# Order of narrow products, a later value product, and two reordered loads in a two-layer encoder

## The chip, the cores and the metric

The kernel runs on one core of a Trainium2 chip. The metric is the device time of one execution in microseconds (us); lower is better. The time before is 1998.18 us, the median of three runs.

## The reference, cut to what matters

256 tokens of width 2048 pass through two layers. Each layer has a token mixer, four cross-attention heads into 256 memory tokens, an output projection and a squared-ReLU MLP of width 8192. All data is float32.

```
m = rms_norm(mem, mem_norm); h = x
for i in range(2):
    n = rms_norm(h, attn_norm[i])
    if i == 0:   q, k, v, qm = split(n @ a_w_in)   # 12 heads, neighbourhood attention + bias
    else:        q, k, v, qm = split(n @ b_w_in)   # 12 query heads on 4 key/value heads,
                                                   # q, k RMS-normed per head, then rotary
    km, vm = split(m @ w_mem_kv[i])                # 4 cross-attention heads
    h = h + concat(mix, cross) @ w_o[i]
    n = rms_norm(h, mlp_norm[i])
    h = h + square(relu(n @ w_up[i])) @ w_down[i]
return rms_norm(h, final_norm)
```

In the first layer each query sees all 4 grid rows and 16 of the 64 columns. The kernel reorders the tokens column by column, so that the 128 queries of a row tile need only 160 neighbouring keys. These are the narrow heads.

## The kernel before, in words

**Numbers.** Every float32 operand is split in two: `hi` is the value rounded by ScalarE to the matrix engine's format (fp32r), `lo` is the rest, computed by VectorE (`split`, lines 484 to 487). A product of two operands is three matmuls: hi x hi, hi x lo, lo x hi.

**Work and its units.** Weights come in chunks of 1 MB, and each chunk is worked off in two half chunks (`halves_of`). There are two kinds. In an S chunk the weights are the stationary operand and a product streams 256 columns (`products`, line 391, 24 products a half chunk, sums `ps_s`, or `ps_u` in the MLP). In an M chunk the activations are stationary and a product streams 512 columns (`m_products`, lines 368, 371, 372, 12 products a half chunk, sums `ps_m`). For each half chunk ScalarE and VectorE make `hi` and `lo` from `raw`, the loaded weights.

**Order.** `run_all` goes through the half chunks one by one. A counter, `tick`, advances after each, and `later(n, f)` runs `f` that many half chunks on; so the attention steps are put in between the projection products. Loads and splits are issued some half chunks ahead. The order in which the functions issue their instructions is then rearranged for each engine by the framework's own scheduler, which works with simulated times and data dependences. `pin` keeps a DMA or instruction in program order; `issue_after(x)` holds what is issued inside it behind instruction `x`. Each engine executes its own queue in order.

**First layer.** The stage begins with the memory's keys and values of both layers. Meanwhile `x_load` (line 826) loads x into `h` and x transposed into two `xT` tiles, four transfers on SyncE's queue. `x_norm` converts xT into `nT` (ScalarE line 516, VectorE line 517, 16 each), and `x_stats` (line 835) squares x on ScalarE and sends the inverse norms around by DMA as `x_row`. Then come the four cross-attention query heads, and three groups of four narrow heads. A group is one value block (4 M chunks) and then a query chunk and a key chunk (S) for each head. When the key chunk of a head is done, `a_k_done` plans the head's steps: scores (`attend_near`), turning the probabilities (`turned_near`), splitting them (`halved`), and the value product (`attend3_near`) 1, 2, 4 and 6 half chunks later. Scores and value product are two pairs of matmuls each: one with 320 columns (both halves of the moving operand, hi as weights) and one with 160 (hi moving, lo as weights), that add up in the same sum. The last head's value product has three 160-column matmuls instead of a pair.

**Second layer.** Queries come in three blocks of four heads (`b_q_done`). `normed_heads` norms them and applies the rotary positions, for the two row tiles i = 0, 1 of 128 tokens: ScalarE scales (lines 1482, 1488), VectorE does six operations (lines 1490, 1496, 1498). TensorE then transposes the result (`heads_T`, line 1453), and scores, softmax (`attend`, with the reciprocal in line 553) and value products of the heads follow, in between products of the output projection.

Of the kernel before, what the change touches and what calls it, by code (L numbers as in the profile page):

```python
# [14 lines left out]
ALU = mybir.AluOpType  # L15
# [143 lines left out]
def encoder_kernel(ctx: ExitStack, tc: tile.TileContext, t: dict, out: bass.AP):  # L159
# [374 lines left out]
    def attend(qT, kT):  # L534
        kT = kT if isinstance(kT, Far) else Near(kT)
        sc_ps = at.att.tile([P, NT, SEQ], F32, tag="att", name="sc_ps")
        for s in range(NT):
            i = NT - 1 - s
            qh, ql = qT[:, i * P : (i + 1) * P], qT[:, SEQ + i * P : SEQ + (i + 1) * P]
            kh, kl = kT.part(0), kT.part(1)  # L540
            ps = kT.out(sc_ps[:, s, :])
            nc.tensor.matmul(ps, qh, kh, start=True, stop=False)  # L542
            nc.tensor.matmul(ps, qh, kl, start=False, stop=False)  # L543
            nc.tensor.matmul(ps, ql, kh, start=False, stop=True)  # L544
        sc = at.work.tile([P, NT, SEQ], F32, tag="sc", bufs=3 + box["layer"], name="sc")
        nm = small.tile([P, NT], F32, tag="nm", name="nm")
        sm = small.tile([P, NT], F32, tag="sm", name="sm")
        nc.vector.tensor_reduce(nm, sc_ps, axis=AX.X, op=ALU.max, negate=True)
        for s in range(NT):
            nc.scalar.activation(sc[:, s, :], sc_ps[:, s, :], AF.Exp, bias=nm[:, s : s + 1],  # L550
                                 accum_out=sm[:, s : s + 1])
        rs = small.tile([P, NT], F32, tag="rs", name="rs")
        nc.vector.reciprocal(rs, sm)
        for s in range(NT):
            nc.vector.tensor_scalar(sc[:, s, :], sc[:, s, :], rs[:, s : s + 1], None, op0=ALU.mult)
        return sc
# [44 lines left out]
    def attend_near(q, k, bias):  # L601

        kk = k.rearrange("p (b t) -> p b t", b=2)
        sc = at.work.tile([P, NT, NEAR], F32, tag="sc", bufs=3, name="sc")
        nm = small.tile([P, NT], F32, tag="nm", name="nm")
        sm = small.tile([P, NT], F32, tag="sm", name="sm")
        for i in range(NT):
            ps = at.att.tile([P, 2, SEQ], F32, tag="att", name="sc_ps")
            s = slice(i * STEP, i * STEP + NEAR)
            nc.tensor.matmul(ps[:, :, :NEAR], q[:, i * P : (i + 1) * P], kk[:, :, s], start=True, stop=False)  # L610
            nc.tensor.matmul(ps[:, 0, :NEAR], q[:, SEQ + i * P : SEQ + (i + 1) * P], kk[:, 0, s], start=False, stop=True)
            nc.vector.tensor_tensor(sc[:, i, :], ps[:, 0, :NEAR], bias[:, i * NEAR : (i + 1) * NEAR], op=ALU.add)
            nc.vector.tensor_tensor(sc[:, i, :], ps[:, 1, :NEAR], sc[:, i, :], op=ALU.add)
        nc.vector.tensor_reduce(nm, sc, axis=AX.X, op=ALU.max, negate=True)
        for i in range(NT):
            nc.scalar.activation(sc[:, i, :], sc[:, i, :], AF.Exp, bias=nm[:, i : i + 1], accum_out=sm[:, i : i + 1])
        rs = small.tile([P, NT], F32, tag="rs", name="rs")
        nc.vector.reciprocal(rs, sm)
        for i in range(NT):
            nc.vector.tensor_scalar(sc[:, i, :], sc[:, i, :], rs[:, i : i + 1], None, op0=ALU.mult)  # L620
        return sc
# [26 lines left out]
    def attend3_near(pT, v, head, cat):  # L648
        av = at.att.tile([P, 2, SEQ], F32, tag="att", name="av")
        for k in range(NT):  # L650
            q, s = slice(k * STEP, k * STEP + NEAR), slice(k * NEAR, (k + 1) * NEAR)
            if head < NH - 1:
                nc.tensor.matmul(av[:, :, q], v(0, k), pT[:, :, s], start=k == 0, stop=False, skip_group_check=True)
            else:
                for n in range(2):
                    nc.tensor.matmul(av[:, 0, q], v(0, k), pT[:, n, s], start=k == n == 0, stop=False,
                                     skip_group_check=True)
            box["av"] = nc.tensor.matmul(av[:, 0, q], v(1, k), pT[:, 0, s], start=False, stop=k == NT - 1,
                                         skip_group_check=True)
        if head == NH - 1:  # L660
            box["cat", head] = split(cat[:, head, :SEQ], cat[:, head, SEQ:], av[:, 0, :])
            return
        y = at.work.tile([P, SEQ], F32, tag="av_s", name="av_s")
        nc.scalar.activation(y, av[:, 1, :], AF.Copy)
        nc.vector.tensor_tensor(y, av[:, 0, :], y, op=ALU.add)
        box["cat", head] = split(cat[:, head, :SEQ], cat[:, head, SEQ:], y)
# [157 lines left out]
        along_free(box["mem_col"], box["mem_row"])  # L824

    def x_load():
        for i in range(NT):
            pin(nc.sync.dma_start(h[:, i, :], t["x"][i * P : (i + 1) * P, :]))
        box["xT"] = []
        for a in range(2):  # L830
            y = at.work.tile([P, 8, SEQ], F32, tag="l4", name="xT")
            pin(nc.sync.dma_start(y.rearrange("p a b -> p (a b)"), t["xT"][:, a * XW // 2 : (a + 1) * XW // 2]))
            box["xT"].append(y)

    def x_stats():
        ss = small.tile([P, NT], F32, tag="ss0", name="x_ss")
# [36 lines left out]
    def a_k_done(hd):  # L873
        def f(w):
            k = at.work.tile([P, 512], F32R, tag="b_y2", name="kT")
            s = summed(w.ps, "k", box["x_row"])
            split(k[:, :SEQ], k[:, SEQ:], s)
            b = at.work.tile([P, NT * NEAR], F32, tag="b_o", bufs=3, name="bias")
            nc.sync.dma_start(b, t["bias"][hd])
            attention([(box.pop(("q", hd)), k, b, head_of(box["v", hd // GH], hd % GH), hd, box["cat"])], 1,  # L880
                      steps=(0, 1, 3, 5 if hd < NH - 1 else 4))
        return f

    def a_qm_done(hd):
# [587 lines left out]
        hi, lo = (dst[:, :, n * SEQ : (n + 1) * SEQ].rearrange("p k (c j) -> p k c j", j=32) for n in range(2))  # L1472
        split(hi, lo, box["q_raw"].rearrange("p t a k j -> p k (t a) j"))

    def normed_heads(w):
        cg, sg = box["rope"]
        outs = []
        for i in range(NT):
            y2 = at.work.tile([P, 4, HD], F32, tag="b_y2", name="b_y2")
            ss = small.tile([P, 4], F32, tag="b_ss", name="b_ss")  # L1480
            for j in range(4):
                nc.scalar.activation(y2[:, j, :], w.ps[i][:, j * HD : (j + 1) * HD], AF.Square,
                                     scale=box["rstd"][:, i : i + 1], accum_out=ss[:, j : j + 1])
            r = rstd_of(ss, HD, "b_r")
            nc.gpsimd.tensor_scalar(r, r, box["rstd"][:, i : i + 1], None, op0=ALU.mult)
            y = at.work.tile([P, 4, HD], F32, tag="b_y", name="b_y")
            for j in range(4):
                nc.scalar.activation(y[:, j, :], w.ps[i][:, j * HD : (j + 1) * HD], AF.Copy, scale=r[:, j : j + 1])
            o = at.work.tile([P, 4, HD], F32, tag="b_o", bufs=2, name="b_o")
            nc.vector.tensor_tensor(o, y, cg[:, i, None, :].to_broadcast([P, 4, HD]), op=ALU.mult)  # L1490
            yv = y.rearrange("p h (a b c) -> p h a b c", a=2, b=2)
            y2v = y2.rearrange("p h (a b c) -> p h a b c", a=2, b=2)
            sv = sg[:, i, :].rearrange("p (a b c) -> p a b c", a=2, b=2)
            for a in range(2):
                for b in range(2):
                    nc.vector.tensor_tensor(y2v[:, :, a, b, :], yv[:, :, a, 1 - b, :],
                                            sv[:, None, a, b, :].to_broadcast([P, 4, 32]), op=ALU.mult)
            nc.vector.tensor_tensor(o, o, y2, op=ALU.add)
            outs.append(o.rearrange("p a b -> p (a b)"))
        return outs  # L1500

# [11 lines left out]

    def b_q_done(blk):
        def f(w):
            outs = normed_heads(w)
            qT = at.work.tile([P, 4, 512], F32R, tag="l4", name="qT1")
            if blk == 0:
                later(1, queries_far, outs)
                later(3, queries_split, qT)  # L1520
            else:
                later(1, heads_T, outs, 4, qT)
            kvs = [(blk * 4 + j) // (NH // NKV) for j in range(4)]
            attention([(qT[:, j, :], Far(box["kT"], kv), None, head_of(box["vb"], kv), blk * 4 + j, box["cat"])
                       for j, kv in enumerate(kvs)], 1 if blk else 3, 2, (0, 3, 6) if blk else (0, 2, 5, 6),
                      2 if blk == 2 else 0)
# [44 lines left out]
    later(21, x_load)  # L1571
    for j in range(8):
        later(24 + j, x_norm, j)
    later(25, x_stats)
    run_all()
    assert not pending, pending
    closed(*reversed(list(pools)))
# [148 lines left out]
```

## Time and profile before

| | |
|---|---|
| median of 3 runs | 1998.18 us (1997.32 to 1998.4) |
| profiled execution, whole | 1997.71 us |
| profiled execution, span from first to last instruction | 1995.6 us |
| TensorE products | busy 1987.0 us, 12870 products |
| TensorE weight loads | busy 1805.0 us |
| VectorE | busy 1717.4 us |
| ScalarE | busy 1327.9 us |
| mean granted TensorE clock | 0.999 |

Engines in the profile are PE (TensorE products), PEld (its weight loads, one for each product, that run beside the products), DVE (VectorE), ACT (ScalarE), POOL (GpSimd) and SP (SyncE, which only issues DMAs). L391 is line 391 of the kernel. A row of the timeline has the start, the time, engine, line, operation, output and inputs, shapes and a count; matmuls are pipelined, so the time from one start to the next says what a product costs, and its own duration is longer than that. The shapes of a product end in its moving columns (128x320).

### The profile page before, as it was taken

Reading aid. Unit: us, or ns where it says so; the run is one execution under the profiler, and the core shown is the slowest. Engines: PE = TensorE matmul, PEld = TensorE weight load, DVE = VectorE, ACT = ScalarE, POOL = GpSimd, SP = SyncE. Lnnn points to the kernel's source line nnn. Section 1 sums busy time; section 2 is a strip of 40 time slices with the busy share of each in tenths; the row PEclk is TensorE's granted clock in tenths of the full one; section 3 lists DMA queues with packets and bytes.
Section 4 is the critical chain, followed back from the end, with each engine's and each line's share of the span. In section 5 each row is a group of like instructions: output and inputs, shape, how many; then the busy total and the mean of one; then the engine's idle time right before and its main releaser. Section 6 shows DMA issues by size and latency. Waiting matters only on the chain.

```text
span 1995.6 us, 32767 instructions
## 1 busy us (share of the span) xinstructions
PE 1987.0 (100%) x12870; PEld 1805.0 (90%) x12870; DVE 1717.4 (86%) x2147; ACT 1327.9 (67%) x1860; POOL 138.2 (7%) x179
## 2 busy tenths in 40 slices
PE   9999999999999999999999999999999999999998
PEld 8999999899999999999998888889999999999997
DVE  7777767589898999999999779778998999999997
ACT  6655555477777777677676656667776777777674
POOL 0000000000000000000000001000000000000000
PEclk9999999999999999999999999999999999999999
DMA  7856555767777777777766764567777777777772
GB/s 294 317 195 201 198 192 184 265 200 233 239 232 226 232 232 237 237 227 231 213 227 209 261 223 150 197 192 259 228 223 240 224 229 236 235 236 227 226 234 107
DMA packets 112731, 446.42 MB, mean 224 GB/s; under 512 B 24128, under 2 KB 45376, under 8 KB 65216
## 3 DMA queue, kind: packets, MB, share of 16 engines
q1 hardware_dynamic: 94560, 413.02, 59.0%
q0 software_dynamic: 17728, 30.78, 9.6%
q8 instruction: 101, 1.65, 0.3%
q10 hardware_dynamic: 288, 0.52, 0.1%
q14 instruction: 54, 0.44, 0.1%
HBM read 397.78 MB, written 4.19 MB: 201 GB/s over the span
## 4 chain that ended last, share of the span: by engine, by line
PE 98%; ACT 1%; DVE 0%; issue 0%; DMA 0%; SPq 0%; DVEq 0%; POOLq 0%; POOL 0%; ACTq 0%
PE ps_u L391 35%; PE ps_s L391 9%; PE p L1183 9%; PE p L1181 9%; PE p L1184 9%; PE ps_m L371 8%; PE ps_m L372 8%; PE ps_m L368 8%; DVE nT L517 0%; PE sc_ps L544 0%; PE sc_ps L543 0%; PE sc_ps L542 0%; PE av L679 0%; PE av L678 0%; PE av L680 0%
## 5 line engine op out<-in xcount | busy, mean ns | idle before, releaser
L391 PE MATMUL ps_u<-hT,uh 128*128 128x256 f32 x3812 | 663.6, 277 | 0.0
L391 PEld LDWEIGHTS ps_u<-hT,uh 128*128 128x128 f32 x3812 | 579.1, 188 | 5.5
L391 PE MATMUL ps_u<-hT,ul 128*128 128x256 f32 x1960 | 542.2, 277 | 0.0
L486 ACT ACTIVATE uh<-raw_U 128x1024 fp32r<-128x1024 f32 x262 | 276.7, 1058 | 205.5 <-PE ps_u L391 192.6
L391 PEld LDWEIGHTS ps_u<-hT,ul 128*128 128x128 f32 x1960 | 368.2, 188 | 0.0
L487 DVE TENSOR_TENSOR lo<-raw,hi 128x1024 fp32r<-128x1024 f32 (+1 forms) x215 | 254.0, 1188 | 92.1 <-ACT hi L486 91.2
L487 DVE TENSOR_TENSOR ul<-raw_U,uh 128x1024 fp32r<-128x1024 f32 x262 | 318.3, 1219 | 14.9 <-ACT uh L486 14.8
L487 DVE TENSOR_TENSOR tl<-t,th 128x2048 fp32r<-128x2048 f32 x116 | 265.6, 2289 | 71.9 <-ACT th L486 71.5
L486 ACT ACTIVATE hi<-raw 128x1024 fp32r<-128x1024 f32 (+1 forms) x215 | 221.7, 1037 | 157.4 <-PE ps_m L372 87.1
L486 ACT ACTIVATE th<-t 128x2048 fp32r<-128x2048 f32 x116 | 222.7, 1920 | 118.8 <-PE p L1184 115.6
L487 DVE TENSOR_TENSOR bl<-b,bh 128x1536 fp32r<-128x1536 f32 x116 | 203.1, 1751 | 0.0
L1181 PE MATMUL p<-th,a_s 128*128 128x512 f32 x464 | 181.4, 391 | 0.0
L1183 PE MATMUL p<-tl,a_s 128*128 128x512 f32 x464 | 181.1, 390 | 0.0
L1184 PE MATMUL p<-th,a_s 128*128 128x512 f32 x464 | 180.7, 389 | 0.0
L1150 POOL DMA_DIRECT2D t<-b x116 | 100.6, 868 | 1144.3 <-ACT t L1149 1060.9
L486 ACT ACTIVATE bh<-b 128x1536 fp32r<-128x1536 f32 x116 | 172.4, 1486 | 7.8
L391 PE MATMUL ps_s<-nT,hi 128*128 128x256 f32 x896 | 155.9, 279 | 0.0
L1184 PE MATMUL p<-bh,a_s 128*128 128x512 f32 x348 | 136.3, 392 | 0.0
L391 PEld LDWEIGHTS ps_s<-nT,hi 128*128 128x128 f32 x896 | 135.8, 188 | 0.2
L1183 PE MATMUL p<-bl,a_s 128*128 128x512 f32 x348 | 135.8, 390 | 0.0
L1181 PE MATMUL p<-bh,a_s 128*128 128x512 f32 x348 | 135.6, 390 | 0.0
L391 PE MATMUL ps_s<-nT,lo 128*128 128x256 f32 x448 | 125.3, 280 | 0.0
(312 smaller groups left out, 3585.6 us busy)
## 6 DMA issues: line engine op xcount, KB each, us to landing
raw_U<-in_w_up SPq DMA_DIRECT2D x128, 1024.0 KB, 5.9
b<-in_w_pair SPq DMA_DIRECT2D x116, 1024.0 KB, 5.8
raw<-in_w_o SPq DMA_DIRECT2D x32, 1024.0 KB, 5.0
t<-b POOLq DMA_DIRECT2D x116, 256.0 KB, 5.2
raw<-in_w_b SPq DMA_DIRECT2D x21, 1024.0 KB, 5.2
raw<-in_w_av SPq DMA_DIRECT2D x12, 1024.0 KB, 5.0
raw<-in_w_aq SPq DMA_DIRECT2D x12, 1024.0 KB, 5.0
raw<-in_w_ak SPq DMA_DIRECT2D x12, 1024.0 KB, 4.9
```

Source lines behind the costliest of these rows:

```text
L368: first = nc.tensor.matmul(ps, ah, hi[:, s], start=st, stop=False)
L371: nc.tensor.matmul(ps, ah, lo[:, s], start=False, stop=False)
L372: final = nc.tensor.matmul(ps, al, hi[:, s], start=False, stop=sp)
L391: ins = nc.tensor.matmul(ps, x, acts[:, k, part], start=k == n == 0, stop=k == KT - 1 and n == 2)
L486: first = nc.scalar.activation(dst_hi, src, AF.Copy)
L487: return first, nc.vector.tensor_tensor(dst_lo, src, dst_hi.bitcast(F32), op=ALU.subtract)
L1150: nc.gpsimd.dma_start(s[:, 3, :], b[:, 1, :], accum_op=ALU.add)
L1181: ins = nc.tensor.matmul(ps, a[:, 0, ai, :], hi[:, s], start=begins, stop=False)
L1183: nc.tensor.matmul(ps, a[:, 0, ai, :], lo[:, s], start=False, stop=False)
L1184: nc.tensor.matmul(ps, a[:, 1, ai, :], hi[:, s], start=False, stop=ends)
```

## The change

Four edits:

1. In `attend_near` and `attend3_near` the 160-column product of each pair is issued before the 320-column one, and now begins the sum. (In the last head it goes before the two that replace the 320-column one.)
2. The value product of heads 3 and 7, the last of a group, comes 10 half chunks after the key chunk and not 6. Head 11 keeps its place.
3. `x_load` issues the two transfers of xT before the two of x, and `x_stats` is planned for tick 28, not 25.
4. In the last query block of the second layer the six rotary operations of row tile 1 on VectorE are held behind the reciprocal that was issued last, the one of head 7's softmax.

```diff
 def attend(...)
-        nc.vector.reciprocal(rs, sm)
+        box["divided"] = nc.vector.reciprocal(rs, sm)
 def attend_near(...)
-            nc.tensor.matmul(ps[:, :, :NEAR], q[:, i * P : (i + 1) * P], kk[:, :, s], start=True, stop=False)
-            nc.tensor.matmul(ps[:, 0, :NEAR], q[:, SEQ + i * P : SEQ + (i + 1) * P], kk[:, 0, s], start=False, stop=True)
+            nc.tensor.matmul(ps[:, 0, :NEAR], q[:, SEQ + i * P : SEQ + (i + 1) * P], kk[:, 0, s], start=True, stop=False,
+                             skip_group_check=True)
+            nc.tensor.matmul(ps[:, :, :NEAR], q[:, i * P : (i + 1) * P], kk[:, :, s], start=False, stop=True,
+                             skip_group_check=True)
 def attend3_near(...)
+            nc.tensor.matmul(av[:, 0, q], v(1, k), pT[:, 0, s], start=k == 0, stop=False, skip_group_check=True)
             if head < NH - 1:
-                nc.tensor.matmul(av[:, :, q], v(0, k), pT[:, :, s], start=k == 0, stop=False, skip_group_check=True)
+                box["av"] = nc.tensor.matmul(av[:, :, q], v(0, k), pT[:, :, s], start=False, stop=k == NT - 1,
+                                             skip_group_check=True)
             else:
                 for n in range(2):
-                    nc.tensor.matmul(av[:, 0, q], v(0, k), pT[:, n, s], start=k == n == 0, stop=False,
-                                     skip_group_check=True)
-            box["av"] = nc.tensor.matmul(av[:, 0, q], v(1, k), pT[:, 0, s], start=False, stop=k == NT - 1,
-                                         skip_group_check=True)
+                    box["av"] = nc.tensor.matmul(av[:, 0, q], v(0, k), pT[:, n, s], start=False,
+                                                 stop=k == NT - 1 and n == 1, skip_group_check=True)
 def x_load()
-        for i in range(NT):
-            pin(nc.sync.dma_start(h[:, i, :], t["x"][i * P : (i + 1) * P, :]))
         box["xT"] = []
         ...
+        for i in range(NT):
+            pin(nc.sync.dma_start(h[:, i, :], t["x"][i * P : (i + 1) * P, :]))
 def a_k_done(hd)
-                      steps=(0, 1, 3, 5 if hd < NH - 1 else 4))
+                      steps=(0, 1, 3, 4 if hd == NH - 1 else 9 if hd % GH == GH - 1 else 5))
-    def normed_heads(w):
+    def normed_heads(w, behind=None):
         ...
+            with tc.issue_after(behind.ins) if behind and i else nullcontext():
+                turned_by_place()        # the six rotary operations, as before
 def b_q_done(blk)
-            outs = normed_heads(w)
+            outs = normed_heads(w, box["divided"] if blk == 2 else None)
 ...
-    later(25, x_stats)
+    later(28, x_stats)
```

More of the change, by code (lines that the diff above doesn't have):

```diff
@@ L1489, in normed_heads, with turned_by_place @@
             o = at.work.tile([P, 4, HD], F32, tag="b_o", bufs=2, name="b_o")
[L1490 to L1498, printed above, removed]
+            def turned_by_place():
+                nc.vector.tensor_tensor(o, y, cg[:, i, None, :].to_broadcast([P, 4, HD]), op=ALU.mult)
+                yv = y.rearrange("p h (a b c) -> p h a b c", a=2, b=2)
+                y2v = y2.rearrange("p h (a b c) -> p h a b c", a=2, b=2)
+                sv = sg[:, i, :].rearrange("p (a b c) -> p a b c", a=2, b=2)
+                for a in range(2):
+                    for b in range(2):
+                        nc.vector.tensor_tensor(y2v[:, :, a, b, :], yv[:, :, a, 1 - b, :],
+                                                sv[:, None, a, b, :].to_broadcast([P, 4, 32]), op=ALU.mult)
+                nc.vector.tensor_tensor(o, o, y2, op=ALU.add)
+            with tc.issue_after(behind.ins) if behind and i else nullcontext():
+                turned_by_place()
             outs.append(o.rearrange("p a b -> p (a b)"))
```

## The prediction

> **What bounds the kernel now.** I read the page first: busy time, then the chain that ended last.
>
> ```profile
> span 1995.6 us, 32767 instructions
> PE 1987.0 (100%) x12870; PEld 1805.0 (90%) x12870; DVE 1717.4 (86%) x2147; ACT 1327.9 (67%) x1860; POOL 138.2 (7%) x179
> PE 98%; ACT 1%; DVE 0%; issue 0%; DMA 0%; SPq 0%; DVEq 0%; POOLq 0%; POOL 0%; ACTq 0%
> ```
>
> TensorE is never out of work for more than a moment: the chain is 98% its own. So an edit counts only where it changes how long a product takes or where a product waits. The change touches the first layer's narrow heads (144 to 355 us), the load of x (54 to 80 us) and the last query block of the second layer (1220 to 1280 us); the two MLPs hold most of the span and stay as they are. What can be won is what the products there lose against their best rhythm.
>
> The second view is the chain in order of time in the narrow heads' stage. Each row is an uninterrupted run of projection products (256 columns): start, time, count.
>
> ```profile
> 94.89 9.07 PE ps_s L391 x80
> 144.34 15.87 PE ps_s L391 x140
> 160.69 10.93 PE ps_s L391 x96
> 172.74 11.22 PE ps_s L391 x95
> 185.32 5.60 PE ps_s L391 x49
> 214.30 16.49 PE ps_s L391 x140
> 243.33 11.22 PE ps_s L391 x95
> 284.89 16.49 PE ps_s L391 x140
> ```
>
> Divide time by count. The same instruction has two rhythms: 113.4 ns (15.87/140), 113.9 and 114.3, against 118.1 (11.22/95) and 117.8 (16.49/140). A run keeps its rhythm to the end. The borders between runs are the narrow heads' products, and there the timeline of the PE shows what changes it:
>
> ```profile
> 171.87 0.24 PE L611 MATMUL sc_ps<-kT,qT 128*128 128x160 f32 x1
> 171.94 0.32 PE L391 MATMUL ps_s<-nT,lo 128*128 128x256 f32 x1
> 172.10 0.31 PE L653 MATMUL av<-pT_n,va 128*128 128x320 f32 x1
> 172.24 0.24 PE L658 MATMUL av<-pT_n,va 128*128 128x160 f32 x1
> 172.32 0.35 PE L653 MATMUL av<-pT_n,va 128*128 128x320 f32 x1
> 172.50 0.24 PE L658 MATMUL av<-pT_n,va 128*128 128x160 f32 x1
> 213.79 0.24 PE L658 MATMUL av<-pT_n,va 128*128 128x160 f32 x1
> 213.87 0.43 PE L372 MATMUL ps_m<-hi,nT 128*128 128x512 f32 x1
> 214.14 0.28 PE L391 MATMUL ps_s<-nT,lo 128*128 128x256 f32 x1
> ```
>
> Read starts, not durations. A 320-column product takes 0.14 (172.10 to 172.24), a 160-column one 0.07 (172.24 to 172.32), but the product behind a 160-column one is about 0.04 late: 320 columns take 0.18 (172.32 to 172.50), 256 columns 0.16 (171.94 to 172.10), 512 columns 0.27 (213.87 to 214.14). The weight loads say why:
>
> ```profile
> 172.25 0.19 PEld L653 LDWEIGHTS av<-pT_n,va 128*128 128x128 f32 x1
> 172.36 0.19 PEld L658 LDWEIGHTS av<-pT_n,va 128*128 128x128 f32 x1
> ```
>
> These two loads enclose the 160-column product of 172.24 and start 0.11 apart: 0.07 of product cannot hide 0.11 of load. What follows the lateness is the slow rhythm: after the block at 172.5 the next 95 products run at 118 ns, and the run of 140 behind the late 512-column product of 213.87 does too, while the run of 140 at 144.34, with no narrow block ahead, runs at 113.4.
>
> **The change part by part**, against the profiled execution's own 1997.71 us (1995.6 of span and 2.1 around it). The median of the runs, 1998.18, is 0.47 above it; I add that at the end. A measurement of this kernel tells about 0.2%, 4.0 us, from no change.
>
> *160-column products first.* No product, load or transfer is added. A block goes from 320, 160, 320, 160 to 160, 320, 160, 320: still two products behind a 160-column one, two times 0.04, so the direct cost is the same. What can change is the rhythm afterwards, because a late 320-column product now stands last, where a late projection product followed. Best case: no run behind a block is slow, and the three runs of 95 (one in each group of four heads) fall from 11.22 to about 10.82 (95 x 113.9 ns): -1.2. Worst: a late wide product hands the slow rhythm on, as the 512-column one at 213.87 did; then the runs of 96 and of 49 become slow too, (96 + 49) x 4.2 ns x 3 = +1.8. The nearest row is 213.87, a wide product as well, which speaks for the loss; but of the three places where projection products directly follow a block (160.5, 172.6, 185.2) only one stayed slow, so the order of the products after it decides as well. I take 0 and keep both ends.
>
> The Trainium skill (TensorE: Matmul & The Clock Gate, section LDWEIGHTS) puts a load at its 128 columns over 1.2 GHz, 107 ns; the 0.11 between the two load rows agrees. By that rule alone a 160-column product uncovers its successor's load wherever it stands, and this edit gives 0.
>
> *A group's last value product four half chunks on.* Heads 3 and 7. Their four products, ScalarE's copy, VectorE's sum and the split into `cat` move; nothing else is queued for them before the output projection, and the value tile they read is asked for again only a group later. The block stands one product ahead of the first projection run (213.4 to 213.9). Four half chunks of 24 products later it falls about 96 products into that run of 140. The first 96 then start behind undisturbed 512-column products, as at 144.34: (16.49 - 15.87)/140 = 4.4 ns each, 0.42 a run, 0.85 for two. If the remaining 44 stay fast as well it is 0.62 a run, 1.24. A gain of nothing, if something other than the block makes those runs slow, is kept as a rival. I take -1.0.
>
> *Transposed input first.* Four 1 MB transfers swap places on SyncE's queue; nothing is added. The stall that this concerns is at 78 us:
>
> ```profile
> L828 SPq DMA_DIRECT2D first<-in_x x2: 477/606/734, 54.4 to 55.2; - x2
> L832 SPq DMA_DIRECT2D xT<-in_xT x2: 473/522/572, 55.7 to 56.3; - x2
> DMA to landing us min/median/max: 10.7/11.6/12.5
> L525 POOL DMA_DIRECT2D x_row<-rows x4: 720/721/743, 72.4 to 74.6; - x4
> L516 ACT ACTIVATE nT<-xT,first 128x256 fp32r<-128x256 f32 x16 | 6.5, 495 | 0.0
> L840 ACT ACTIVATE sq<-first 128x512 f32<-128x512 f32 x8 | 4.9, 618 | 0.0
> 76.22 2.00 ACT L486 ACTIVATE hi<-raw 128x1024 fp32r<-128x1024 f32 x2
> 77.47 2.34 DVE L487 TENSOR_TENSOR lo<-raw,hi 128x1024 fp32r<-128x1024 f32 x2
> 77.94 0.62 PE L368 MATMUL ps_m<-hi,memT 128*128 128x512 f32 x2
> 78.73 0.50 PE L371 MATMUL ps_m<-lo,memT 128*128 128x512 f32 x1 [0.17 <-DVE lo L487]
> ```
>
> Two products start from 77.94 at the usual 0.23, so the next was due at 78.40; it starts at 78.73 and takes 0.50, not 0.39: about 0.45 lost. It waited for `lo`, that for `hi` at 76.22, which stood in ScalarE's queue behind the 16 conversions of xT. xT first lets these begin earlier; the squares of x come after them, with three half chunks more until they are due. Gain between 0.45 (conversions out of the way) and 0 (the eight squares take their place ahead of the same `hi`; VectorE, which has no squares, still finds `lo` sooner). A loss is bounded by the row of inverse norms: its transfers were issued at 72.4 to 74.6, and it is first used behind the projection products that begin at 94.9; three half chunks of 24 products, some 2.7 us each, leave about 10 us. I take -0.3.
>
> *Last rotary products held.* VectorE's rotary work of the last query block's second half (row tile i = 1) must now follow the reciprocal of head 7:
>
> ```profile
> 1231.56 0.68 DVE L1490 TENSOR_TENSOR b_o<-b_y,cos_q 128x512 f32<-128x512 f32 x1
> 1232.16 0.68 DVE L1496 TENSOR_TENSOR b_y<-b_y,sin_q 128x128 f32<-128x128 f32 x3
> 1234.39 1.21 DVE L487 TENSOR_TENSOR lo<-raw,hi 128x1024 fp32r<-128x1024 f32 x1
> 1235.59 0.68 DVE L1498 TENSOR_TENSOR b_o<-b_o,b_y 128x512 f32<-128x512 f32 x1
> 1235.65 0.50 PE L371 MATMUL ps_m<-lo,cat 128*128 128x512 f32 x1
> 1250.26 0.17 DVE L553 RECIPROCAL rs<-sm 128x2 f32<-128x2 f32 x1 [0.22 <-ACT sc L550]
> 1252.10 2.39 DVE L487 TENSOR_TENSOR lo<-raw,hi 128x1024 fp32r<-128x1024 f32 x2 [0.69 <-ACT hi L486]
> 1252.19 0.60 PE L1453 MATMUL pt_h<-ident,b_o 128*128 128x128 f32 x4
> ```
>
> Gain: the `lo` of 1234.39 ends just before TensorE's product of 1235.65, which takes about 0.11 more than 0.39. Without 1.4 us of rotary products ahead of it that wait goes: -0.1, and it is all there is to win. Cost: the six operations (0.68, four within 0.9, 0.68: about 2.2) start after 1250.4 and end near 1252.6 at best; the transposes that read them stand at 1252.19, 0.4 late. At worst they stand behind the two `lo` of 1252.10 and the transposes come at 1256.2, 4.0 late. Queued behind the held work on VectorE are those two `lo`; behind the transposes the scores, softmax and value products of heads 8 to 11. TensorE meanwhile has output-projection products of finished heads, as in this stretch now. I take 0 for the cost, with 4.0 as the other end.
>
> Sum: 0 - 1.0 - 0.3 - 0.1 = -1.4: 1996.3 in a profile, 1996.8 as a median.
>
> **The rivals.**
>
> *The new order clears every run.* For it: the runs that start after blocks recover in two cases of three. Against it: 213.87. -1.2 - 1.24 - 0.45 - 0.1 = -3.0: median 1995.2.
>
> *A late wide product hands the slow rhythm on.* For it: 214.14 behind 213.87. +1.8 - 0.85 - 0.3 - 0.1 = +0.55: median 1998.7.
>
> *The rhythm does not hang on the blocks*, so the two edits on them do nothing: -0.4, median 1997.8. The Trainium skill (SBUF — State Buffer, section Who interferes with whom) gives TensorE two independent read ports and says that it waits on nobody; by that, the two read streams could not disturb each other. The rows of 113.4 and 117.8 ns for one instruction are not explained by it, so it gets little.
>
> *The held rotary work delays the last heads* (slower). Place: transposes at 1252.19. Price: up to 4.0, with the other gains kept 1997.7 - 1.4 + 4.0 = 2000.3, median 2000.8; without them 2002.2. It decides once the delay exceeds the output products that TensorE has ready beside the last heads; up to that point it costs nothing.
>
> **How the numbers follow.** Chances: forecast 0.43, all runs cleared 0.22, rhythm handed on 0.17, no effect 0.08, rotary delay 0.10. The range leaves out half of the rotary case and the far end of the clearing one: 1994.8 to 1999.8. Faster by over 4.0 us needs under 1994.2, 1.0 below the best case: 0.06. Slower by as much needs the full rotary delay and no gain: 0.05. The rest, 0.89, is no difference that can be told.
>
> **What would show it.** The chain's runs from 214 and 285 us should read 96 products at 113.4 ns each, with a narrow block behind them; if they stay at 118, the second edit failed. Runs of 95 at 118 again: order neutral; at 114: the clearing rival; runs of 96 or 49 at 118: the handing-on one. At 78 us no product should start late. TensorE should show no wait on the split of `qT` or on `cat` between 1250 and 1282; a wait there, or a schedule that reorders the products in some other place, makes the forecast wrong.

## The result and the profile after

| | before | after |
|---|---|---|
| median of 22 runs each | 1998.36 us | 1994.92 us |
| lowest to highest | 1997.31 to 1999.45 | 1993.94 to 1996.71 |
| ratio, 95% interval | | 0.9984 (0.9978 to 0.999) |
| profiled execution, whole | 1997.71 us | 1995.76 us |

The kernel is 3.4 us faster (0.17%). That is real, since the interval ends below 1, but it is inside the 4 us that the prediction counted as no change. The forecast of 1996.8 was 1.9 us too high; the range (1994.8 to 1999.8) held by only 0.12 us. Page of after, busy time and chain:

```profile
span 1993.9 us, 32782 instructions
PE 1984.5 (100%) x12870; PEld 1802.1 (90%) x12870; DVE 1715.7 (86%) x2147; ACT 1327.4 (67%) x1860; POOL 137.4 (7%) x179
PE 99%; DMA 0%; issue 0%; ACT 0%; SPq 0%; DVE 0%; DVEq 0%; POOLq 0%; POOL 0%; ACTq 0%
```

The same 12870 products now keep TensorE busy 2.5 us less. So the gain is in how long products take, not in work. To find the place, I cut three executions at the same TensorE products (first product with x, first query product and so on) and took the difference of their starts. The third column is a second profile of the changed kernel, e5 below.

| stage, us | before | after | after, e5 |
|---|---|---|---|
| first product to first M product | 23.16 | 23.50 | 23.05 |
| rest of the memory's keys and values | 66.30 | 65.83 | 65.83 |
| cross-attention queries, first value block | 49.45 | 49.45 | 49.45 |
| narrow heads, later value blocks | 187.75 | 186.39 | 185.65 |
| output projection | 88.87 | 88.89 | 88.89 |
| MLP | 660.32 | 660.30 | 660.10 |
| second layer's mixer and output | 246.62 | 246.49 | 246.49 |
| MLP | 660.38 | 660.39 | 660.38 |
| end | 7.49 | 7.50 | 7.49 |

Three stages moved, and they are those that the edits touch: 0.47, 2.10 (e5) and 0.13. The first MLP is scatter: it takes 660.10 to 660.69 over the fourteen profiles of this study, whatever edits they have. The first line varies without any reason in the code: from 22.87 to 24.09 over the same profiles. The stages must therefore be compared, and not the spans. The narrow heads' stage repeats well: 187.75 in before, e3, e4 and e9, which have the same code there. Line numbers of after are a little higher: the 160-column products are L610 (scores) and L654 (values), the 320-column ones L612 and L656.

The chain of after in order of time, narrow heads, runs of 256-column products (start, time, count):

```profile
144.11 14.51 PE ps_s L391 x128
158.81 1.20 PE ps_s L391 x10
160.29 9.78 PE ps_s L391 x86
172.49 9.53 PE ps_s L391 x84
184.69 5.68 PE ps_s L391 x50
213.27 2.73 PE ps_s L391 x24
216.51 11.80 PE ps_s L391 x104
286.94 11.80 PE ps_s L391 x104
```

Divide again: 113.4, 113.7, 113.5, 113.6, 113.8, 113.5. No long run at 118 ns is left. Two further things are new. Each pair of projection runs has a run of 10 between (120 ns each, with one late product in it), and the value product of the heads 3 and 7 stands 24 products into its run, not 96. The timeline of PE between 169.9 and 172.5 shows what the runs of 10 are:

```profile
169.90 0.35 PE L610 MATMUL sc_ps<-kT,qT 128*128 128x160 f32 x2
170.09 0.32 PE L391 MATMUL ps_s<-nT,lo 128*128 128x256 f32 x1
171.28 0.46 PE L612 MATMUL sc_ps<-kT,qT 128*128 128x320 f32 x2
171.58 0.23 PE L654 MATMUL av<-pT_n,va 128*128 128x160 f32 x1
171.65 0.44 PE L391 MATMUL ps_s<-nT,hi 128*128 128x256 f32 x2
171.93 0.31 PE L656 MATMUL av<-pT_n,va 128*128 128x320 f32 x1
172.07 0.24 PE L654 MATMUL av<-pT_n,va 128*128 128x160 f32 x1
172.15 0.35 PE L656 MATMUL av<-pT_n,va 128*128 128x320 f32 x1
172.33 0.28 PE L391 MATMUL ps_s<-nT,lo 128*128 128x256 f32 x1
172.45 0.39 PE L391 MATMUL ps_s<-nT,hi 128*128 128x256 f32 x2
```

A block is no longer one piece. The 160-column product streams only `hi`, which ScalarE makes first; put first in its pair, it no longer waits for VectorE's `lo`, and the scheduler issues it earlier: two score products ten projection products ahead of the other two, a value product two to four ahead. The last product of the block is the late 320-column one (172.15 to 172.33, 0.18), and the projection products behind it run at 113.5.

The two other places, timelines of after. At 78 us, where `lo` had been waited for, products follow each other at 0.22 to 0.23:

```profile
78.18 0.61 PE L368 MATMUL ps_m<-hi,memT 128*128 128x512 f32 x2
78.63 0.39 PE L371 MATMUL ps_m<-lo,memT 128*128 128x512 f32 x1
78.86 0.39 PE L372 MATMUL ps_m<-hi,memT 128*128 128x512 f32 x1
```

And in the second layer VectorE makes the third `lo` of that stretch without row tile 1's rotary work ahead of it; the held work and the transposes come later:

```profile
1231.59 0.13 DVE L553 RECIPROCAL rs<-sm 128x2 f32<-128x2 f32 x1
1231.63 1.21 DVE L487 TENSOR_TENSOR lo<-raw,hi 128x1024 fp32r<-128x1024 f32 x1
1249.68 0.69 DVE L1502 TENSOR_TENSOR b_o<-b_o,b_y 128x512 f32<-128x512 f32 x1
1252.69 0.82 PE L1455 MATMUL pt_h<-ident,b_o 128*128 128x128 f32 x6
```

The waits of PE have no row between 1248 and 1284 us. One wait is there that before's profile did not have:

```profile
252.94 0.46 PE L612 MATMUL sc_ps<-kT,qT 128*128 128x320 f32 x2
253.33 0.47 ACT L486 ACTIVATE pT_n<-pT_n 128x320 fp32r<-128x320 f32 x1 [3.89 <-DMA pT_n<-sc_t]
253.85 0.34 PE L654 MATMUL av<-pT_n,va 128*128 128x160 f32 x1 [0.46 <-ACT pT_n L486]
```

Head 6's turned probabilities came late by DMA, and TensorE lost 0.73 us here. This is why the narrow heads' stage of after is longer than that of e5, which has no such wait. The first of these transfers took 5.2 us from issue to landing, and 3.1 in e5, which is the same program. Nor is the wait the change's own: e2 and e10 below keep the old order of the blocks and wait here too (1.06 and about 0.5).

### The profile page after: what moved, and what is told of

The parts are those of the page before. It is cut to its first block, busy times and chain, and to the rows that moved or that the text cites. A ratio compares the mean times of both kernels' runs of the same rounds, so it can differ in the third digit from the quotient of the medians.

```text
span 1993.9 us, 32782 instructions
## 1 busy us (share of the span) xinstructions
PE 1984.5 (100%) x12870; PEld 1802.1 (90%) x12870; DVE 1715.7 (86%) x2147; ACT 1327.4 (67%) x1860; POOL 137.4 (7%) x179
## 4 chain that ended last, share of the span: by engine, by line
PE 99%; DMA 0%; issue 0%; ACT 0%; SPq 0%; DVE 0%; DVEq 0%; POOLq 0%; POOL 0%; ACTq 0%
PE ps_u L391 35%; PE ps_s L391 10%; PE p L1185 9%; PE p L1183 9%; PE p L1186 9%; PE ps_m L368 8%; PE ps_m L372 8%; PE ps_m L371 8%; PE sc_ps L544 0%; PE sc_ps L543 0%; PE sc_ps L542 0%; PE av L681 0%; PE av L682 0%; PE av L680 0%; DMA first<-in_mem_rest 0%
```

## Experiments

The stages and runs below come from one profile of each kernel. The times of e1 to e7 are medians of eleven runs, beside the median of before's. e8 to e12 ran once each (1998.45, 1998.27, 1999.05, 1999.80 and 2000.01 us, with 1998.32, 1997.28 for three of them, and 1998.50 for before beside them); these times tell nothing alone, and only the profiles are read.

**e1, edit 1 alone.** Before with the new order in `attend_near` and `attend3_near`, nothing else.

> Edit 1 alone. Theory A (a narrow block that ends in a 160-column product leaves the slow rhythm of 118 ns behind, one that ends in a 320-column product does not, so this edit alone cures the runs of 95 and the runs of 140 behind the value product of heads 3 and 7): all projection runs between 144 and 331 us at 113.4 to 114 ns, 2.4 us less than before in the time. Rival B (each edit has its own share: this one cures only the three runs of 95, the move of the value product cures the two runs of 140): 1.2 us less, and the runs of 140 still at 118 ns.

1996.99 us against 1997.83 (ratio 0.9996, 0.9987 to 1.0005). The intervals of e1 to e4 all include 1, so what each edit is worth is read from its stage. The narrow heads' stage: 186.81, 0.94 less. Its chain:

```profile
143.91 14.51 PE ps_s L391 x128
172.29 9.54 PE ps_s L391 x84
213.60 15.08 PE ps_s L391 x128
283.87 15.08 PE ps_s L391 x128
```

The run that was the one of 95 is fast (113.6). The runs behind the value blocks of heads 3 and 7 stay slow (117.8), new order or not. So edit 1 does nearly half of the stage's gain. Where a projection product directly follows the late 320-column product, nothing is handed on. Ahead of the two runs at 117.8 ns, two 512-column products stand between. Timeline of PE:

```profile
212.79 0.35 PE L656 MATMUL av<-pT_n,va 128*128 128x320 f32 x1
212.98 0.39 PE L371 MATMUL ps_m<-lo,nT 128*128 128x512 f32 x1
213.21 0.39 PE L372 MATMUL ps_m<-hi,nT 128*128 128x512 f32 x1
213.44 0.28 PE L391 MATMUL ps_s<-nT,lo 128*128 128x256 f32 x1
```

The 320-column product takes 0.185 here as well, and the two behind it 231 and 230 ns, by the unrounded starts; the two ahead of the run that starts at 143.75 (113.4 ns) take 227 and 226. So here the block's lateness may have been handed on through them; no run separates that from the mere nearness of the block to the border.

**e2, edit 2 alone.**

```diff
-                      steps=(0, 1, 3, 5 if hd < NH - 1 else 4))
+                      steps=(0, 1, 3, 4 if hd == NH - 1 else 9 if hd % GH == GH - 1 else 5))
```

> Edit 2 alone. In the instruction order the block of heads 3 and 7 now stands behind the first 24 projection products of the run, with the 320-column product still ahead of its 160-column one, and the projection goes on with a product on hi weights, as at 172.5 us before. Theory A: the 24 are fast, the other 116 stay at 118 ns, 0.2 us less. Rival B: the 116 are fast too, 1.2 us less.

1996.89 us against the same 1997.83 (0.9995, 0.9987 to 1.0004).

```profile
173.43 11.22 PE ps_s L391 x95
214.47 2.73 PE ps_s L391 x24
217.68 13.20 PE ps_s L391 x116
```

Here the run of 95 stays slow and the 140 products behind 214 are fast: 113.8 ns for 24 and for 116. The stage is 187.67 with a wait of 1.06 for head 6's probabilities in it, 186.61 without: 1.14 less. The two gains add up: 0.94 + 1.14 = 2.08, and e5 has 2.10. The run of 116 began with a `hi` product and is fast, so resuming on `hi` does not make a run slow.

**e8, the block right at the border.** Before, with the value product of heads 3 and 7 nine half chunks after the key chunk (`8 if hd % GH == GH - 1` in place of 9 above), which puts it between the last M product and the first projection product.

> The kernel before, with the value product of heads 3 and 7 three half chunks later, which in the instruction order moves it past a single product: it stands directly ahead of the projection run, behind the last 512-column product. Theory E (the slow rhythm is set off among 512-column products and carried over the border; behind a block that stands directly ahead of 256-column products it ends within a few): the two runs of 140 at 114 ns, 1.2 us less in the stage. Rival F (a block right at the start of a run makes it slow, wherever the 512-column product stands): still 118 ns.

The PE timeline at the border, then the chain's two runs behind such borders:

```profile
215.02 0.24 PE L658 MATMUL av<-pT_n,va 128*128 128x160 f32 x1
215.10 0.32 PE L391 MATMUL ps_s<-nT,lo 128*128 128x256 f32 x1
```

```profile
215.26 16.53 PE ps_s L391 x140
285.84 16.53 PE ps_s L391 x140
```

118.1 ns, and the stage as before (187.73). The late 512-column product that the prediction took as the messenger is not needed: a block next to the border, with or without M products between, leaves the run slow. 24 products into it (e2) it doesn't.

**e11, the border's special half chunk taken away.** The kernel before splits the first half chunk of a run behind M chunks in its own way (`entered_half`): its first product is a `lo` product, and that product's weights lie elsewhere in the tile. Here that half chunk is split like the others.

> The kernel before, in which the half chunk that follows from an M chunk to an S chunk gets its hi and lo parts by the ordinary split and not by the special one for such borders; other data placement and other times of the conversions at each such border, no product more or less. Theory G (the slow rhythm of a run that follows a narrow block at the border hangs on when and where the first half chunk of that run is converted): the runs of 140 at 214 and 285 us read 113 to 114 ns a product, or the run at 144 us becomes slow too. Rival (only the narrow block ahead of the run matters): 144 us stays at 113 to 114 ns and the runs at 214 and 285 us stay at 117 to 119. A gain or loss elsewhere is no evidence for either.

```profile
145.78 16.49 PE ps_s L391 x140
216.37 16.49 PE ps_s L391 x140
```

The run at 144 us, which no block precedes, turns slow as well: 117.8. The stage is 188.39, 0.64 longer, of which (16.49 - 15.87) is 0.62. So a run behind M chunks is slow by itself, the special half chunk cures it, and a block at the border undoes the cure. This schedule differs in other places too, so e12 changes less.

**e12, the place of the weights alone.**

```diff
-        self.rest = room[:, STILL_AT // 4 :][:, : HALF - P]
-        self.first = room[:, (STILL_AT + ENTRY_AT) // 4 + HALF - P :][:, :P]
+        self.first = room[:, STILL_AT // 4 :][:, :P]
+        self.rest = room[:, STILL_AT // 4 + P :][:, : HALF - P]
```

> The kernel before with one thing changed at the borders from M to S chunks: the first 128 columns of that half chunk's lo part stay where an ordinary split has them, at the front of the tile, where the kernel before puts them at the tile's end, 192 bytes further on. TensorE's order, every shape and VectorE's split into two pieces stay. Theory P (the place in SBUF of the weights that the first product of the run reads decides whether the run starts in the fast rhythm): the run at 144 us reads 117 to 119 ns a product, 16.4 to 16.6 us for 140, as in the run without the special half chunk, and the stage gets 0.6 us longer. Rival O (the order decides: the special half chunk starts with its lo product): the run at 144 us stays at 113 to 114 ns, 15.8 to 15.9 us for 140. In both, the runs at 214 and 285 us, behind their narrow blocks, stay at 117 to 119 ns.

```profile
145.84 16.49 PE ps_s L391 x140
216.43 16.49 PE ps_s L391 x140
```

The instructions of TensorE, VectorE and ScalarE and their order are those of before; only the addresses in SBUF differ, of the first 128 columns of `lo` (and the rest, which makes room for them). The run at 144 us goes from 113.4 to 117.8 ns and the stage to 188.39; the cross-attention queries, also behind M chunks, take 49.84 instead of 49.45. The 512-column products ahead of the run follow each other at 225 to 227 ns, as in before (226 to 228). So where no block stands ahead the place decides, not the order. The Trainium skill (SBUF — State Buffer, section Who interferes with whom) lists two independent read ports for TensorE, one for the moving operand and one for weight loads, and no place in memory that would matter. It does not explain these rows, and the measurement decides.

**e3, edit 3 alone** (order of the four loads, `x_stats` at tick 28).

> Edit 3 alone (both parts: order of the loads, and x_stats at tick 28). Theory A: the late product at 78 us goes and nothing comes in its place, 0.45 us less. Rival B: it only moves, because the squares of x take the place of the conversions on ScalarE, 0.1 us less or nothing.

1997.75 us against 1997.83 (0.9998, 0.9989 to 1.0007): nothing that its time can tell. But its profile has no wait at 78 us,

```profile
78.31 0.62 PE L368 MATMUL ps_m<-hi,memT 128*128 128x512 f32 x2
78.77 0.39 PE L371 MATMUL ps_m<-lo,memT 128*128 128x512 f32 x1
```

and the rest of the memory's stage is 65.83, as in all five profiles with this edit; without it, and with the border as it was, seven profiles have 66.30 to 66.61. With either order of the loads the tick leaves the order of instructions on every engine as it was (this is read from the programs; no run has the tick alone), so the order of the loads does all of it.

**e4, edit 4 alone.**

> Edit 4 alone. Theory A: the late product at 1235.65 goes, the rest of the last query block stays as it is, 0.15 us less between 1216 and 1327 us. Rival B: the transposes of the last block come later and TensorE waits for the last heads: slower by 0.4 to 4 us. Rival C: more than 0.5 us less, because the freed VectorE lets the heads of the second block come earlier.

1997.49 us against 1997.83 (0.9999, 0.999 to 1.0008). The second layer's mixer stage is 246.45, 0.17 under before's. That is the tenth predicted. But e1 and e2, which do not contain edit 4, wait longer at the same place. Timeline of e1, then of e2:

```profile
1235.15 1.22 DVE L487 TENSOR_TENSOR lo<-raw,hi 128x1024 fp32r<-128x1024 f32 x1
1236.42 0.50 PE L371 MATMUL ps_m<-lo,cat 128*128 128x512 f32 x1 [1.11 <-DVE lo L487]
```

```profile
1236.77 0.50 PE L371 MATMUL ps_m<-lo,cat 128*128 128x512 f32 x1 [0.39 <-DVE lo L487]
```

**e5, e6 and e7: the changed kernel again, without edit 4, and with the other heads' value products moved too** (`else 7` in place of `else 5` for the heads inside a group).

> The changed kernel once more, for a second profile and for the comparison with the two beside it. Theory C (two places hang on how an execution falls: the value product of head 6, which in the profile of the change waits 0.7 us for a landing, and VectorE's lo at 1230 to 1236 us, which the change has cured): the wait at 253 us is there or not, none over 0.3 us at 1228 to 1240; 2.5 to 3.5 us less than before. Rival D (the profile's wait at 253 us is fixed): it is 0.6 to 0.8 us again.

> The change without edit 4 (the rotary products of the last block are not held). Theory C (VectorE has no idle time at 1227 to 1240, so its lo comes late by an amount that differs from execution to execution, and the held work takes it away): TensorE waits for lo in that stretch, 0.5 to 2 us in the profile, and the time is 0.5 to 2 us above the changed kernel beside it. Rival D (the prediction's value of edit 4, 0.1): within 0.2 us of it.

> The changed kernel, and the value products of the other narrow heads (not the last of a group, not head 11) two half chunks later than in it, some 25 projection products on. Theory C: no wait for the landing of the turned probabilities is left (0.7 us at 253 us in the change's profile), the projection runs stay at 113.5 ns, and the time is 0.2 to 0.7 us below the changed kernel beside it. Rival D: a block of value products inside a run sets off the slow rhythm again, and 0.4 us a group is lost.

Against 1998.32: e5 1994.52 (0.9982, 0.9973 to 0.9991), e6 1995.61 (0.9988, 0.9979 to 0.9997), e7 1994.85 (0.9983, 0.9974 to 0.9992). e5 is 3.8 under before, a little more than the 2.5 to 3.5 expected, and has no wait at 253 us, so that wait comes and goes between executions. Leaving edit 4 out costs 1.1 us between the medians. All eleven runs of e6 lie above e5's median; but the two intervals overlap, and e6's profile has no wait near 1235 (stage 246.47), so that this is a strong hint and not more. e7 keeps every run fast (x30 in 3.43, x57 in 6.48) and is no faster than e5, where 0.2 to 0.7 us had been expected, so a looser plan for the other heads gains nothing.

**e9 and e10: a delay on purpose.** Three extra copies on ScalarE, 1.8 us together, ahead of the norm of the last query block; e9 in the kernel before, e10 with edit 4 added.

> The kernel before, with three extra copies of 128x512 on ScalarE (about 0.6 us each, 1.8 us together) put ahead of the norm of the last query block of the second layer; their results are overwritten. They stand in for a DMA landing that comes late and makes ScalarE's conversions, and with them VectorE's chain at 1226 to 1236 us, late. Theory (edit 4 is insurance: it takes 1.4 us of VectorE's work out of the way of the weights' lo part, so that a late chain does not reach TensorE): TensorE waits 1.2 to 2.0 us for lo between 1228 and 1240 us, where the execution of before waited 0.16. Rival (TensorE has enough converted weights there, so the chain's delay does not reach it, and the waits of e1 and e2 had another cause): no wait over 0.3 us there.

> The kernel before with the same three extra copies on ScalarE and with the fourth edit (rotary work of row tile 1 held). Theory (insurance): the wait for lo between 1228 and 1240 us is at least 0.9 us smaller than in the run with the delay alone, 0 to 0.7 us. Rival (the held rotary work does not shorten the chain to lo): the same wait as in the run with the delay alone, within 0.3 us.

Timeline of e9, then of e10:

```profile
1234.18 0.91 DVE L1501 TENSOR_TENSOR b_y<-b_y,sin_q 128x128 f32<-128x128 f32 x4
1234.99 1.24 DVE L487 TENSOR_TENSOR lo<-raw,hi 128x1024 fp32r<-128x1024 f32 x1
1236.28 0.50 PE L371 MATMUL ps_m<-lo,cat 128*128 128x512 f32 x1 [0.49 <-DVE lo L487]
```

```profile
1235.05 0.15 DVE L553 RECIPROCAL rs<-sm 128x2 f32<-128x2 f32 x1
1235.13 1.20 DVE L487 TENSOR_TENSOR lo<-raw,hi 128x1024 fp32r<-128x1024 f32 x1
```

With the delay TensorE waits 0.49 us; with edit 4 on top it doesn't wait. The direction is that of the insurance theory, the sizes are not: a wait of 1.2 to 2.0 had been expected for e9 and a saving of at least 0.9 for e10. Only 0.6 of the 1.8 us reached `lo`, probably because ScalarE had been waiting for a DMA there anyway (this was not tried apart). Nor is the delay all that differs: the extra copies changed the order of TensorE's products in this stage from 1225 us on, and of VectorE's work ahead of `lo`. Put into one table, with the end of this third `lo` and the stage counted from the first M product of the second layer (1081.12 us in before, whose `lo` ends at 1235.60):

| kernel | end of third `lo` | stage |
|---|---|---|
| e4 (edit 4) | 153.04 | 246.45 |
| after (edit 4) | 153.31 | 246.49 |
| e5 (edit 4) | 153.35 | 246.49 |
| e7 (edit 4) | 153.61 | 246.45 |
| e10 (edit 4, delay) | 153.73 | 246.46 |
| e3 | 154.17 | 246.49 |
| e6 | 154.31 | 246.47 |
| e8 | 154.39 | 246.52 |
| before | 154.48 | 246.62 |
| e12 | 154.82 | 246.99 |
| e2 | 154.99 | 247.16 |
| e9 (delay) | 155.09 | 247.17 |
| e1 | 156.61 | 248.74 |

Up to about 154.3 the end of `lo` costs nothing; beyond, each microsecond costs about one. Before stood on that edge. Its execution happened to lose 0.13; e1's lost 2.3, in two waits, when ScalarE stood idle for 2.83 us ahead of the conversion of the turned probabilities (`pT_t`), which waits for a DMA to land; in before it was 0.62. The last transfer that this conversion needs was issued 1.0 us later in the stage than in before and took 4.5 us to land, not 3.2. (e11 is not in the table. Its `lo` ends at 154.55 and costs it 0.06 more than before's, which fits; but its stage of 247.16 loses another 0.46 near its end, at 1325 us, where a second `lo` comes late.) Edit 4 moves `lo` about 1 us away from the edge. Of a loss like e1's it could take back about that much, as an estimate from the table; no run shows it.

## Why the prediction was right or wrong

**Verdict, bound, place: right.** No difference over 0.2%, TensorE the bound, all gain that the stages show at the three places named, no price for the held rotary work (its transposes begin 173.2 us into the stage, 1252.69 - 1079.53, where before they stood at 171.1, and TensorE waits for nothing there). That the range held as well is partly luck: the median lies 0.12 us above its lower end.

**The size: 1.4 was forecast, the stages give 0.94 + 1.14 + 0.47 + 0.13 = 2.7,** and the medians 3.4 with an interval of 2.0 to 4.4. By terms:

- *160-column products first, taken as 0, measured 0.94.* This is the step that failed. The direct cost was right, and so were both ends. But between the ends I chose by the row at 213.87, the late 512-column product, and read it as a wide product that hands the slow rhythm on. e8 has the 118 ns without such a product, and in after a late 320-column product stands directly ahead of runs at 113.5 ns. The row was evidence for "next to the border with the M products", not for "late and wide". I also expected a block to stay in one piece. The rule of the Trainium skill quoted there gave 0 as well: its account of the load fits the late products, but the 0.94 lies in the rhythm of the runs that follow, of which it says nothing.
- *Value product later, taken as 1.0, measured 1.14.* Right, with a wrong place: 24 products into the run, not 96. I counted four half chunks from where the block stood; the plan counts from the key chunk, and the eight half chunks that follow it are M chunks, so ten lie two half chunks at most into the run.
- *Transposed input first, taken as 0.3, measured 0.47.* The squares did not take the conversions' place; the upper end was the value.
- *Rotary held, taken as -0.1.* Right for the execution that was profiled, too small as a term: the wait at this place was 0.13 in that one and 0 to 2.3 in others without edit 4, which moves `lo` by about 1. One execution was read as if it were every one.

**The rivals.** The clearing one (1995.2) is the nearest; it put the whole 1.2 on edit 1, which brought 0.94. "The rhythm does not hang on the blocks" falls with e1 and e2, "handed on", as it was priced (runs of 96 and 49 slow), with e1, the rotary delay with the missing wait.

**Still open.** Why a place in SBUF sets the rhythm, and why the run of 95 was slow while those of 96 and 49, behind blocks of the same products, were not: place and lateness may act together there, but no run separated them. The same holds for the two runs of e1 at 117.8 ns. Also open is some 0.7 us between the stages' 2.7 and the medians' 3.4. A part may be late `lo` in executions that no profile shows; the interval admits that there is nothing to explain.

## What to carry to other kernels

When TensorE is the bound, divide the time of each uninterrupted run by its count before looking for waits: a second rhythm of the same instruction is a loss that no wait shows, and moving the interruption, or the weights, can remove it. Put first the member of a pair whose operands are ready first, since the scheduler can then take the pair apart. A chain that ends exactly when it is needed is worth more than its wait in one profile: measure its slack over several executions.

## What the runs showed of the hardware

The same 256-column product has two stable rhythms, 113.4 to 113.9 and 117.8 to 118.1 ns, kept over up to 140 products until something interrupts them. Which one starts can hang on where in SBUF the weights of the run's first half chunk lie: same instructions, same order, 15.87 against 16.49 us for 140. And identical code starts unevenly: the stretch from the first product to the first M product took 22.87 to 24.09 us, more than any of the four edits is worth.
